# Values as the stationary operand, 64 columns a head, with attention outputs kept on chip in a one-core hybrid layer

## The chip, the cores and the metric

The kernel runs on one core of a Trainium2 chip. The metric is the device time of one execution in microseconds (us). The kernel before took 1282.35 us in the median of three runs (1281.9 to 1283.98). For one more execution the profiler recorded every instruction; all rows quoted below come from that one.

A core has five engines with a queue of instructions each, which the profile names PE (TensorE, matrix products), DVE (VectorE), ACT (ScalarE), POOL (GpSimd) and SP (SyncE, which here only issues DMAs). ACT issues some DMAs too. An engine executes its queue in order and waits on semaphores for others. A matrix product is two instructions on PE: a load of the stationary operand (PEld, LDWEIGHTS) and the streaming of the moving operand through it (PE, MATMUL). Results go to PSUM.

## What is computed

The layer has a convolution branch, an attention branch and a gated merge. The change lies in the attention branch, whose reference is this:

```python
scores = jnp.einsum('bdhnqe,bdhnke->bdhnqk', qb, kb) * (e ** -0.5)
scores = jnp.where(mask, scores, NEG_INF)
m = jnp.max(scores, axis=-1)
p = jnp.exp(scores - m[..., None])
den = jnp.sum(p, axis=-1)
o = jnp.einsum('bdhnqk,bdhnke->bdhnqe', p, vb) / den[..., None]
...
m_all = jnp.maximum(jnp.maximum(maxes[0], maxes[1]), maxes[2])
wts = [d_g * jnp.exp(m_g - m_all) for m_g, d_g in zip(maxes, dens)]
w_sum = wts[0] + wts[1] + wts[2]
att = (wts[0][..., None] * outs[0] + wts[1][..., None] * outs[1]
       + wts[2][..., None] * outs[2]) / w_sum[..., None]
y_att = (att * jax.nn.silu(z_att)) @ w_att_out[layer]
```

There are 1024 tokens and 24 heads of 64 channels: three groups of eight heads. Group g looks back over a window of 128 steps at a stride of 1, 4 or 16 tokens. Group 0 has one sequence of 1024 tokens, group 1 has four of 256, group 2 sixteen of 64, of which two share a tile of 128 queries. A query tile of 128 attends its own key block and, where there is one, the block before: 256 keys, or 128. The three outputs of a head position are merged by the softmax denominators and row maxima.

## The kernel before

Every float32 operand of a product is split in a high part, which the fast float32 format holds, and a low part, the rest. ACT writes the high part and DVE (or POOL, for some weights) the low one (`split`, L55 to L58). A projection takes three products (`mm3`, L73 to L75).

Attention is done for `order`: 12 units n = (j, g), j a pair of heads (0 to 3), g the group. One unit has two heads and eight query tiles a head; a **stage** is one pair of neighbouring tiles of one head, so a unit has 8 stages and the whole has 96. A loop over **slots** (at the end of `layer`) writes PE's order by hand; a slot is about 3.8 to 4.6 us long. A slot holds, in this order on PE:

- a piece of 12 products of 512 columns of a projection that runs beside attention (`pieces`): k and q of later units, then from slot 85 on the eight gate projections. `Parts` takes k and q out of PSUM with rotary, `gate` takes a gate out with a sigmoid on ACT;
- `scores(st)` of stage st = slot: q stationary, k moving, 2 products a tile. DVE adds the mask and takes the row extremum (L861, written to `ov`), ACT takes the exponential and the row sum (L865);
- `turn` of the stage two slots back (TURN = 2): transposes of the exponentials on PE (L873), then `split` into `ph` and `pl`;
- `values` of the stage three slots back (VAL = 3): for each query tile and key block two products (L886), `ph` and `pl` stationary with 128 columns, and v moving, 128 columns: 64 of the high part and 64 of the low part of one head. A DVE sum (L889) adds the two halves into the tile `ov`, which has tokens on partitions and 66 columns a head: 64 outputs, the sum, the extremum;
- work put into later slots by `beside`.

After the last stage of a unit `o_store` writes `ov` to DRAM (`oscr`), in token order, by ACT's queue. When the three groups of a pair j are there, `combine(j, half)` loads half the tokens back (`rd`, L898), forms the weights, sums the groups on DVE (L910 to L935), transposes the result with four PE transposes (L939) and multiplies it with the SiLU gate, which SP loads (`at`). For j < 3 the product goes to DRAM (`atscr`) and is read back after the last stage; for j = 3 it is split at once (`att_parts`).

`load_v(n)` reads v of one unit from DRAM (`vr`) and splits it in `vt`. `move_kq` moves k and q of a head within SBUF by 32-partition DMAs that SP issues (L794).

PE's order is the one in which the code is written; on DVE, ACT, POOL and SP the framework's scheduler places the instructions by its own estimates of time, within the data's dependences and the tiles' buffers. Each engine then keeps that order on the chip.

## Time and profile before

| what | us |
|---|---|
| three runs, median (lowest, highest) | 1282.35 (1281.9, 1283.98) |
| the profiled execution, own time | 1283.09 |
| its span, first to last instruction | 1281.3 |
| granted TensorE clock, share of full | 0.998 |
| first score product to last value product | 671.0 to 1090.4 |
| last of the gate projections ends | 1141.7 |

A row of the groups reads: line, engine, operation, output<-inputs by tile names, shapes, count | busy us, mean ns of one | idle time before them and what ended it. Matmul durations overlap each other, so a group's busy time is not the time that PE needs for it; that is the spacing from one start to the next, which the timeline shows. In the table of waits a row says who waited for whom, the total in us, how often, and the longest.

### The profile page before, as it was taken

To read this page: it belongs to the slowest core of one execution; us is meant where nothing else is said; L and a number is where in the kernel's file an instruction comes from. 1 tells how busy PE (TensorE), PEld (TensorE's weight loads), DVE (VectorE), ACT (ScalarE), POOL (GpSimd) and SP (SyncE) were. 2 spreads that over 40 slices of the span, in tenths; PEclk is the share of its full clock that TensorE was granted. 3 is DMA by queue.
4 is the path that set the end of the run, shared out by engine and by line. 5 is a ranking of instruction groups with operands and counts; after the bars stand their busy time and mean duration, and the time that the engine had idled before them with its cause. 6 is when DMAs were issued, how large, how long until landed. Compare 5 with 4: busy or idle time off the path is not lost. (4 is left out here: it accounts for less than half of the span.)

```text
span 1281.3 us, 16765 instructions
## 1 busy us (share of the span) xinstructions
PE 1250.6 (98%) x6148; PEld 1050.8 (82%) x6148; DVE 932.8 (73%) x1600; ACT 489.6 (38%) x957; POOL 91.8 (7%) x79
## 2 busy tenths in 40 slices
PE   6999999999999999999999999999999999999997
PEld 4777888888888888888788888888888888788886
DVE  6777999999999986853257667866876854448544
ACT  4653202111221156620125545545545567334211
POOL 0000000000000000000131111111011111100000
PEclk9999999999999999999999999999999999999999
DMA  9522311211211122555665556566565563648321
GB/s 366 189 90 72 109 66 60 89 51 48 92 57 50 50 74 74 166 178 187 147 166 128 149 149 175 151 168 168 152 186 143 152 203 106 205 168 307 100 99 66
DMA packets 85525, 171.52 MB, mean 134 GB/s; under 512 B 11202, under 2 KB 41026, under 8 KB 85444
## 3 DMA queue, kind: packets, MB, share of 16 engines
q1 hardware_dynamic: 69024, 157.66, 40.9%
q10 hardware_dynamic: 16420, 12.80, 3.3%
q8 instruction: 48, 0.79, 0.2%
q14 instruction: 33, 0.27, 0.1%
HBM read 105.74 MB, written 33.23 MB: 108 GB/s over the span
## 5 line engine op out<-in xcount | busy, mean ns | idle before, releaser
L73 PE MATMUL d<-hh,whi 128*128 128x512 f32 x1072 | 424.8, 396 | 1.8 <-ACT gs L740 0.9
L74 PE MATMUL d<-hl,whi 128*128 128x512 f32 x1072 | 417.8, 390 | 2.1 <-DVE hl L347 2.1
L75 PE MATMUL d<-hh,wlo 128*128 128x512 f32 x1072 | 418.1, 390 | 0.0
L406 DVE SCALAR_TENSOR_TENSOR v<-u,cw,v 128x1024 f32<-128x1024 f32 x232 | 280.7, 1284 | 0.0
L75 PEld LDWEIGHTS d<-hh,wlo 128*128 128x128 f32 x1072 | 201.2, 188 | 43.3
L74 PEld LDWEIGHTS d<-hl,whi 128*128 128x128 f32 x1072 | 201.7, 188 | 41.7 <-DVE hl L347 2.9
L73 PEld LDWEIGHTS d<-hh,whi 128*128 128x128 f32 x1072 | 201.6, 188 | 41.4 <-ACT gs L740 1.3
L57 ACT ACTIVATE whi<-wraw 128x512 fp32r<-128x512 f32 (+1 forms) x107 | 88.0, 833 | 252.0 <-PE d L74 227.1
L58 POOL TENSOR_TENSOR wlo<-wraw,whi 128x512 fp32r<-128x512 f32 (+1 forms) x56 | 82.7, 1490 | 668.0 <-ACT whi L57 625.1
L865 ACT ACTIVATE sb<-sb,ov 128x128 f32<-128x128 f32 (+1 forms) x192 | 84.6, 442 | 45.2 <-DVE ov L861 44.8
L861 DVE CUSTOM_DVE_ANT_0 sb<-s,mask 128x128 f32<-128x128 f32 (+1 forms) x192 | 59.8, 347 | 34.3 <-PE s L858 34.1
L58 DVE TENSOR_TENSOR pl<-t,ph 128x384 fp32r<-128x384 f32 (+2 forms) x96 | 52.2, 544 | 29.1 <-ACT ph L57 28.4
L886 PE MATMUL o<-vt,ph 128*128 128x128 f32 x280 | 71.1, 286 | 1.4 <-ACT ph L57 1.2
L886 PE MATMUL o<-vt,pl 128*128 128x128 f32 x280 | 68.1, 277 | 2.9 <-DVE pl L58 2.6
L58 DVE TENSOR_TENSOR wlo<-wraw,whi 128x1024 fp32r<-128x1024 f32 (+1 forms) x51 | 58.0, 1139 | 15.9 <-ACT whi L57 15.3
L57 ACT ACTIVATE ph<-t 128x384 fp32r<-128x384 f32 (+2 forms) x96 | 46.0, 480 | 58.8 <-PE t L873 56.5
L886 PEld LDWEIGHTS o<-vt,pl 128*128 128x128 f32 x280 | 53.7, 192 | 4.5 <-DVE pl L58 4.4
L886 PEld LDWEIGHTS o<-vt,ph 128*128 128x128 f32 x280 | 53.5, 191 | 2.9 <-ACT ph L57 2.8
L1089 PE MATMUL d<-oh,hl 128*128 128x512 f32 (+1 forms) x136 | 51.2, 376 | 0.0
L1087 PE MATMUL d<-oh,hh 128*128 128x512 f32 (+1 forms) x136 | 51.2, 376 | 0.0
L632 DVE TENSOR_TENSOR gs<-d,sgc 128x512 f32<-128x512 f32 x16 | 11.1, 692 | 54.9 <-PE d L75 48.9
L858 PE MATMUL s<-k,ql 128*128 128x128 f32 (+1 forms) x192 | 50.9, 279 | 0.0
(220 smaller groups left out, 1924.0 us busy)
## 6 DMA issues: line engine op xcount, KB each, us to landing
wraw<-in_w_t SPq DMA_DIRECT2D x67, 512.0 KB, 4.3
k<-kqp SPq DMA_DIRECT2D x96, 128.0 KB, 4.0
q<-kqp SPq DMA_DIRECT2D x96, 128.0 KB, 3.4
wa<-in_w_ada SPq DMA_DIRECT2D x16, 512.0 KB, 6.3
rd<-oscr SPq DMA_DIRECT2D x8, 792.0 KB, 4.9
ql<-kqp SPq DMA_DIRECT2D x48, 128.0 KB, 3.1
wraw<-in_w_v SPq DMA_DIRECT2D x11, 512.0 KB, 3.7
x<-in_xT SPq DMA_DIRECT2D x8, 512.0 KB, 10.2
```

The source lines that it names most:

```text
L57: nc.scalar.activation(hi, raw, AF.Copy)
L58: (lo_eng or nc.vector).tensor_sub(lo, raw, hi.bitcast(F32))
L73: nc.tensor.matmul(ps, lh, rh, start=start, stop=False)
L74: nc.tensor.matmul(ps, lh, rl, start=False, stop=False)
L75: nc.tensor.matmul(ps, ll, rh, start=False, stop=stop)
L406: nc.vector.scalar_tensor_tensor(d, u[:, k:k + S], cw[:, ct, k:k + 1], d, op0=mult, op1=add)
L858: nc.tensor.matmul(ps[:, c:c + w], ql[:, ts_], k[:, ks], start=False, stop=True)
L861: nc.vector.tensor_tensor_reduce(out=sb[:, c:c + w], in0=ps[:, c:c + w], in1=mk, scale=-SCALE, scalar=3e38, op0=add, op1=ALU.min, accum_ou ...
L865: nc.scalar.activation(sb[:, c:c + w], sb[:, c:c + w], AF.Exp, bias=ov[:, t, h, 65:66], scale=-1.0, accum_out=ov[:, t, h, 64:65])
L886: nc.tensor.matmul(self.po[:, t % 4], parts[x][:, c + i:c + i + P], v[:, kb], start=i == 0 and x == 0, stop=i + P == w and x == 1)
L1087: nc.tensor.matmul(ps, hh[:, k, c], rh, start=k == 0, stop=False)
L1089: nc.tensor.matmul(ps, hl[:, k, c], rh, start=False, stop=k == KT - 1)
```

## The change

In words:

- **values**: v is now stationary, 64 columns of one head, high or low part; `ph` and `pl` move. Per key block three products, vh·ph, vl·ph and vh·pl, are summed in PSUM; vl·pl is no longer formed. For groups 0 and 1 one key block serves its own query tile and the next, so one product moves 256 columns. The result lies in PSUM with the 64 channels on partitions and the tokens in columns.
- **outputs**: one ACT copy for two stages (64 partitions by 512) puts them into a tile `oc` that holds two heads (partitions 0 to 63 and 64 to 127) by 1024 tokens and stays in SBUF. The DVE sum is gone, and so are `oscr` and the load `rd`.
- **statistics**: sums and extrema lie in a tile `stats`, which ACT's queue stores to `sscr` (16 bytes a token, group and pair). `combine(j)`, once for all 1024 tokens, loads them (`sd`), forms 48 columns of weights, transposes these on PE (one transpose), stores them to `wscr` and loads them back as rows, broadcast over 64 partitions (`wg`, six pairs of loads). The products with the weights run on `oc` in place. Group 1 and 2 are read in token order through the access pattern.
- **buffers**: `wg`, the gate (`gt`), `row`, `w` and `wt` share one tag of two buffers; `oc` has four.
- **v** is loaded and split in two halves of four key blocks each, later than before.
- **order**: VAL is 4, and `values` stands before `turn` in a slot.

The diff, cut:

```diff
+    sscr = [dram.tile([S, 3, 4], F32, name=f"sscr{j}") for j in range(4)]
+    wscr = [dram.tile([3, 2, S], F32, name=f"wscr{j}") for j in range(4)]
...
-    oscr = [dram.tile([S, 3, 2 * 66], F32, name=f"oscr{j}") for j in range(4)]
...
         for h in range(2):
-            v = v2[n, h] = stk.tile([P, 8, P], F32R, name="vt", tag=f"v{turn_of(n, h)}")
-            src = raw[:, :, 64 * h:64 * h + 64]
-            nc.scalar.activation(v[:, :, 0:64], src, AF.Copy)
-            nc.vector.tensor_sub(v[:, :, 64:128], src, v[:, :, 0:64].bitcast(F32))
+            if not half:
+                v2[n, h] = stk.tile([P, 8, 2, 64], F32R, name="vt", tag=f"v{turn_of(n, h)}")
+            hi, lo = (v2[n, h][:, 4 * half:4 * half + 4, x] for x in range(2))
+            split(hi, lo, raw[:, :, 64 * h:64 * h + 64])
             yield
...
         def values(self, st_):
             tp, h, spans, _ = self.spans(st_)
-            parts, v = self.pt.pop(st_), v2[self.n, h]
+            (ph, pl), v = self.pt.pop(st_), v2[self.n, h]
             if st_ % 2 == 0:
-                self.po = psa.tile([P, 4, P], F32, name="o", tag="o")
-            for t, c, w in spans:
-                for i in range(0, w, P):
-                    kb = t - (w - P - i) // P
-                    for x in range(2):
-                        nc.tensor.matmul(self.po[:, t % 4], parts[x][:, c + i:c + i + P], v[:, kb],
-                                         start=i == 0 and x == 0, stop=i + P == w and x == 1)
+                self.po = psa.tile([P, 512], F32, name="o", tag="o")
+
+            c, w = spans[0][2] - P, (1 if self.g == 2 else 2) * P
+            blocks = [(tp, c, w, 0), (tp + 1, c + w, P, P)]
+            if c:
+                blocks.insert(1, (tp - 1, 0, P, 0))
+            for n, (kb, c, w, q) in enumerate(blocks):
+                out_ = self.po[0:64, tp % 4 * P + q:tp % 4 * P + q + w]
...
+                nc.tensor.matmul(out_, v[:, kb, 0], ph[:, c:c + w], start=first_, stop=False)
+                nc.tensor.matmul(out_, v[:, kb, 1], ph[:, c:c + w], start=False, stop=False)
+                nc.tensor.matmul(out_, v[:, kb, 0], pl[:, c:c + w], start=False, stop=last_)
             if st_ % 2:
-                nc.vector.tensor_reduce(self.ov[:, tp - 2:tp + 2, h, 0:64],
-                                        self.po.rearrange("p t (x c) -> p t c x", x=2),
-                                        axis=mybir.AxisListType.X, op=add)
...
+                nc.scalar.activation(self.o[64 * h:64 * h + 64, (tp - 2) * P:(tp + 2) * P], self.po[0:64], AF.Copy)
...
+    def combine(j):
+        sd = ap_.tile([P, 8, 3, 2, 2], F32, name="sd")
+        nc.sync.dma_start(sd.rearrange("p t g h x -> p t (g h x)"), sscr[j].rearrange("(t p) g c -> p t (g c)", p=P))
...
+        nc.scalar.activation(m, m, AF.Exp, scale=-1.0)
...
+        nc.tensor.transpose(pt[0:48, 0:P], w, ident)
+        wt = row_tile("wt")[0:48, 0:P]
+        nc.scalar.activation(wt, pt[0:48, 0:P], AF.Copy)
+        nc.sync.dma_start(wscr[j].rearrange("g h (t p) -> (g h t) p", p=P), wt)
...
+            for h in range(2):
+                nc.sync.dma_start(row[64 * h:64 * h + 64], wscr[j][g, h:h + 1, s].to_broadcast([64, 512]))
...
+        for half, s in enumerate(halves):
...
+            nc.vector.tensor_mul(o0, o0, w0)
+            w2 = row_of(2, s)
+            v = w1.rearrange("p (i r) -> p i r", r=4)
+            nc.vector.tensor_mul(v, v, o1)
+            nc.vector.tensor_add(o0, o0, w1)
+            gt = row_tile("gt")
+            nc.sync.dma_start(gt, zascr[j][:, s])
+            yield
+            v = w2.rearrange("p (i t s) -> p i t s", t=8, s=2)
+            nc.vector.tensor_mul(v, v, o2)
+            nc.vector.tensor_add(o0, o0, w2)
+            nc.vector.tensor_mul(o0, o0, gt)
...
-    LEAD, TURN, VAL = 11, 2, 3
+    LEAD, TURN, VAL = 11, 2, 4
...
-    FIRST, SECOND = (2, 6, 6, 7, 7, 9), (8, 11, 11, 12, 12, 14)
+    STEPS = (2, 3, 4, 5, 7, 8, 9, 10, 11)
```

What it does to PE's order shows in a slot of the fifth unit (j = 1, g = 1), whose stage has three key blocks in all. Before, from the scores on (k and q are the score operands, t the transposes, o the values):

```order
L857 MATMUL s<-k_5847,q_5848 128x128
L858 MATMUL s<-k_5847,ql 128x128
L857 MATMUL s<-k_5847,q_5848 128x256
L858 MATMUL s<-k_5847,ql 128x256
L873 MATMUL t<-ident,sb 128x128 x3
L886 MATMUL o<-vt,ph 128x128
L886 MATMUL o<-vt,pl 128x128
L886 MATMUL o<-vt,ph 128x128
L886 MATMUL o<-vt,pl 128x128
L886 MATMUL o<-vt,ph 128x128
L886 MATMUL o<-vt,pl 128x128
```

Now, from the last score on, for the same pair of tiles:

```order
L863 MATMUL s<-k_5728,ql 128x256
L896 MATMUL o<-ph,vt 64x256
L897 MATMUL o<-ph,vt 64x256
L898 MATMUL o<-pl,vt 64x256
L896 MATMUL o<-ph,vt 64x128
L897 MATMUL o<-ph,vt 64x128
L898 MATMUL o<-pl,vt 64x128
L878 MATMUL t<-ident,sb 128x128 x4
```

The last name in a row is the stationary operand: six products with 128 stationary columns became six with 64, three of them twice as wide in the moving operand, and the transposes moved behind them (they belong to another stage, so their count differs). Over all stages 560 value products of 128 columns became 456 of 128 and 192 of 256, and 32 transposes in `combine` became 4.

The second place is SP's queue in the first `combine` (j = 0), from the first broadcast rows of its first half to its last store; k and q belong to the sixth unit. None of the `wg` rows stood there before; `rd`, `at` and `atscr` did:

```order
L941 DMA wg<-wscr_97 64x512 [waits DMAHW1_49,DMAHW5_49,DMAHW0_49,DVE_49]
L941 DMA wg<-wscr_97 64x512 [waits DMAHW6_49]
L794 DMA k_6154<-kqp 32x1024 [waits DMAHW7_49,DVE_49]
L959 DMA gt<-zascr_89 128x512 [waits DMAHW3_49,DMAHW2_49,DVE_49]
L794 DMA q_6155<-kqp 32x1024 x2
L794 DMA ql<-kqp 32x1024
L941 DMA wg<-wscr_97 64x512 [waits DMAHW5_49,DMAHW6_49,DMAHW4_49,DVE_49]
L941 DMA wg<-wscr_97 64x512
L941 DMA wg<-wscr_97 64x512 [waits DMAHW0_49,DVE_49]
L941 DMA wg<-wscr_97 64x512 [waits DMAHW7_49]
L968 DMA atscr_101<-oc 128x512
```

Each load that reuses a buffer waits for the DVE operation which read it last, and the moves of k and q stand between those waits.

The third place is ACT's queue at the end of the last unit, where the statistics of the last pair are stored and loaded (`ph` are the last exponentials on their way to the values, `gs` a gate projection):

```order
L701 DMA sscr_96<-stats 512x1x4 [waits Activation_49]
L701 DMA sscr_96<-stats 512x1x4
L57 ACTIVATE whi<-wraw 128x1024 [waits DMAHW0_49,PE_49,Pool_49]
L740 ACT_TABLE_LOAD [waits DMAHW5_49]
L740 ACTIVATE gs<-d 128x512 [waits PE_49]
L57 ACTIVATE ph<-t 128x256 [waits PE_49]
L741 DMA ascr<-gs 128x512 [waits Activation_49]
L57 ACTIVATE ah<-wraw 128x512 [waits DMAHW0_49]
L921 ACT_TABLE_LOAD [waits DMAHW2_49]
L921 ACTIVATE sd<-sd 128x48 [waits DVE_49]
L902 ACTIVATE oc<-o 64x512 [waits PE_49]
L57 ACTIVATE ph<-t 128x256 [waits PE_49]
```

The exponential of the merged statistics of the last pair (L921), which waits for a store and a load, now stands ahead of the last `ph` of the program; before, that of the last pair (L916) stood behind all `ph`.

## The prediction

> **What bounds the kernel now.** I began with the totals of the page.

> ```profile
> span 1281.3 us, 16765 instructions
> PE 1250.6 (98%) x6148; PEld 1050.8 (82%) x6148; DVE 932.8 (73%) x1600; ACT 489.6 (38%) x957; POOL 91.8 (7%) x79
> ```

> PE is busy for 98% of the span; no other engine is near. So the time is the number of products times the spacing from one start to the next, plus the few places where PE waits. Next I read PE's timeline of one slot of group 2, for the spacing (start, duration, engine, line):

> ```profile
> 764.10 0.39 PE L75 MATMUL d<-hh,wlo 128*128 128x512 f32 x1
> 764.32 0.22 PE L857 MATMUL s<-k,q 128*128 128x128 f32 x1
> 764.38 0.28 PE L858 MATMUL s<-k,ql 128*128 128x128 f32 x1
> 764.49 0.27 PE L857 MATMUL s<-k,q 128*128 128x128 f32 x1
> 764.61 0.28 PE L858 MATMUL s<-k,ql 128*128 128x128 f32 x1
> 764.72 0.40 PE L873 MATMUL t<-ident,sb 128*128 128x128 f32 x2
> 764.88 0.31 PE L886 MATMUL o<-vt,ph 128*128 128x128 f32 x1
> 765.02 0.27 PE L886 MATMUL o<-vt,pl 128*128 128x128 f32 x1
> 765.13 0.27 PE L886 MATMUL o<-vt,ph 128*128 128x128 f32 x1
> 765.24 0.28 PE L886 MATMUL o<-vt,pl 128*128 128x128 f32 x1
> 765.36 0.45 PE L73 MATMUL d<-hh,whi 128*128 128x512 f32 x1
> ...
> 765.87 0.39 PE L75 MATMUL d<-hh,wlo 128*128 128x512 f32 x1
> 766.10 0.39 PE L73 MATMUL d<-hh,whi 128*128 128x512 f32 x1
> ```

> Products of 512 columns start 0.23 us apart (765.87 to 766.10). The value products, 128 moving columns each with a stationary operand of its own, start 0.11 us apart. But the first score product needed only 0.06 us (764.32 to 764.38): the load of the next operand had been done under the 512 columns ahead. So 128 columns stream in about 58 ns, and what holds the value products at 112 ns is the load of 128 stationary columns. The next timelines, PEld and then a score stage with 256 moving columns, say the same:

> ```profile
> 764.43 0.19 PEld L857 LDWEIGHTS s<-k,q 128*128 128x128 f32 x1
> 764.54 0.19 PEld L858 LDWEIGHTS s<-k,ql 128*128 128x128 f32 x1
> ...
> 766.10 0.19 PEld L74 LDWEIGHTS d<-hl,whi 128*128 128x128 f32 x1
> ```

> ```profile
> 783.74 0.28 PE L857 MATMUL s<-k,q 128*128 128x256 f32 x1
> 783.85 0.28 PE L858 MATMUL s<-k,ql 128*128 128x256 f32 x1
> 783.97 0.28 PE L857 MATMUL s<-k,q 128*128 128x256 f32 x1
> 784.09 0.28 PE L858 MATMUL s<-k,ql 128*128 128x256 f32 x1
> ```

> Loads follow each other at 0.11 us (764.43, 764.54), and 256 moving columns cost 0.12 us, hardly more than 128. Last, the table of PEld's waits in the attention stretch (in all, times, longest):

> ```profile
> PEld o L886 <- DVE pl L58: 4.4, 11, 0.8
> PEld o L886 <- ACT ph L57: 2.8, 6, 1.1
> PEld s L857 <- DVE ov L861: 2.8, 1, 2.8
> PEld d L73 <- ACT gs L740: 1.3, 1, 1.3
> ```

> Most of what PE loses there, 7.2 us, is the value products waiting for `pl` and `ph`.

> **Value products.** Nothing in the trace loads 64 columns. Two rows give load durations for 2 columns and for 128:

> ```profile
> L320 PEld LDWEIGHTS d<-wh,s_parts x8: 83/83/83, 95.8 to 99.0; 128*2 128x2 f32 x8
> L125 PEld LDWEIGHTS d<-ones,tot x32: 188/192/192, 47.4 to 489.2; 128*128 128x128 f32 x32
> ```

> That is (188 - 83) / 126 = 0.83 ns a column; 64 columns fewer take 53 ns off the 112, which leaves 59 ns, as much as the 58 ns of the stream. Bounds for a product of 64 by 128: 57 ns (the stream alone) and 112 ns (no price by column); with 256 moving columns 113 to 120 ns. I take 59 and 120, near the lower end, because the 2-column load, 105 ns shorter, shows that a load does get shorter with its columns. [...]

> By stage, before against after:
> - 24 stages of four blocks: 8 x 112 = 896 ns; now three products of 256 and six of 128, 3 x 120 + 6 x 59 = 714. Saving 182 ns, 4.4 us in all.
> - 40 of three blocks: 6 x 112 = 672; now 3 x 120 + 3 x 59 = 537. Saving 135 ns, 5.4 us.
> - 32 of two blocks (group 2): 4 x 112 = 448; now 6 x 59 = 354. Saving 94 ns, 3.0 us.

> That makes 12.8 us. By the halves of a ns that the rows don't resolve (58 to 66 for the 128) it lies between 13.4 and 9.6; I take **11.4** (62 ns).

> **Transposes in combine.**

> ```profile
> L939 PE MATMUL t<-ident,pr 128*128 128x128 f32 x32 | 4.9, 277 | 0.0
> ```

> These 32 become 4. They too load one operand each, so 28 x 0.11 = **3.1 us** less on PE.

> **The later values.** VAL = 4 leaves `ph` and `pl` one more slot, about 4 us, against waits of 1.1 us at most: I take off all **7.2 us**. What is late next is the pair that the table names besides, the extrema (2.8 us, at the first stage, where k and q arrive) and `gs` (1.3 us); both stay.

> **DVE and ACT.** These are off the path:

> ```profile
> L889 DVE TENSOR_REDUCE ov<-o 128x256 f32<-128x512 f32 x48 | 32.7, 682 | 1.4 <-PE o L886 1.1
> L510 ACT ACTIVATE gs<-d 128x512 f32<-128x512 f32 x24 | 14.2, 592 | 21.8 <-issue 14.5 <-PE d L75 7.3
> L930 DVE TENSOR_TENSOR rd<-rd,w 128x512 f32<-128x512 f32 x24 | 17.4, 777 | 0.0
> ```

> DVE loses the 48 sums, 32.7 us. ACT gains 48 copies out of PSUM, 0.59 us each by the row of `gs` (the same shape), 28 us. The merge itself keeps about its work: twelve products and sums of 128 by 512 a pair at 0.78 us are 9.3 us; before, `rd` alone had 24 / 4 = 6 of them a pair beside other, smaller ones. Strided reads of `oc` may cost more, up to the 1.03 us of the dearest 128x512 operation on DVE, 3 us a pair. I cost this at nothing, since DVE has room; the next windows show it (span, PE, PEld, DVE, ACT, POOL busy, clock, DMA share, GB/s), first between two `combine`s, then where the gates run:

> ```profile
> 772.00:875.00 103.00, 102.14 (x606) 89.50 (x605) 76.17 (x226) 53.57 (x155) 15.33 (x12) 1.00 0.63 167
> 1048.00:1064.00 16.00, 15.49 (x93) 13.15 (x92) 5.77 (x23) 12.87 (x28) 2.40 (x1) 1.00 0.44 124
> ```

> DVE has 103 - 76 = 27 us free. ACT has 49 us free in the first stretch, but only 3.1 of 16 us in the second.

> **SP and the moves.** In the new order SP's queue holds the broadcast rows, `gt` and the moves of k and q, each load waiting for DVE to be done with a buffer. Without k and q I count 28 issues a pair instead of 13.

> ```profile
> 834.16 1.23 SPq L794 DMA_DIRECT2D q<-kqp  x2
> ...
> SPq L942 <- DVE at L940: 24.5, 5, 8.0
> ...
> at<-zascr SPq DMA_DIRECT2D x8, 256.0 KB, 3.6
> row<-bscr SPq DMA_DIRECT2D x8, 64.0 KB, 4.0
> ```

> At 1.23 / 2 = 0.62 us an issue that is 15 x 0.62 = 9 us more of SP's time in about 103 us. SP already stood still for up to 8.0 us behind DVE in `combine`, and no wait of PE for k or q came of it after the first stage. So nothing for that, unless DVE itself gets stuck (below).

> **New waits.** `combine` now makes a chain: `sd` load, DVE, exponential, DVE, PE transpose, store, broadcast load, DVE. A load takes 3.6 to 4.0 us by the rows above. At the end of the last unit the exponential stands ahead of the last `ph` on ACT, behind a store and a load; and `combine`'s DVE rows stand in front of the extrema and of `pl`. Neither has a row in the trace; below, the cost is nothing if the load lands in time; above, one store and one load, about 8 us, less the 4 us which VAL gives. I take **2 us**, the middle; a gain is excluded, because the old order had no such wait.

> **Sum.** The profiled execution took 1283.09 us (span 1281.3 and 1.8 around it). 1283.1 - 11.4 - 3.1 - 7.2 + 2.0 = 1263.4. The median of the runs is 0.7 below the profiled one: **1262.7 us**. With the kindest bounds (13.4 and no new wait) 1258.7; with the waits of the first stage and of `gs` gone as well, 1254.6. With 9.6 and 4 us of waits 1266.5.

> **Rivals.**
> 1. *The load has no price by column.* Then 128 moving columns cost 112 still, and the extra products are a loss: four blocks 3 x 120 + 6 x 112 = 1032 against 896, three 696 against 672, two 672 against 448; 3.3 + 1.0 + 7.2 = 11.5 us more instead of 11.4 less. 1262.7 + 22.9 = 1285.6, and some less where a load hides beside 256 columns: 1281 to 1286, no change to slightly slower. Against it: the 83 ns of L320.
> 2. *Loads don't run under a product whose rows they share.* Each product would take load plus stream: 456 x 0.117 + 192 x 0.179 = 87.7 us instead of 560 x 0.112 = 62.7: 25 more; 1262.7 + 36.4 = 1299. Against it speaks that at 766.10 a load and a 512-column product, both on all 128 rows, start together and products stay 0.23 us apart. [...]
> 3. *DVE gets stuck in `combine`* (slower). Four waits a half for rows or gate, eight a pair, at 4 us: 32 us in which DVE, in order, does neither extrema nor `pl`. `STEPS` spreads `combine` over ten slots, about 42 us at 4.2; there DVE has a quarter free, 11 us, and four of the 0.68 us sums less, 3 us; PE follows some 6 us later by the slots between scores and values. 32 - 11 - 3 - 6 = 12 us a pair, three pairs: 36 us, 1299. It decides once DVE falls over 6 us behind. For it: two buffers for everything, each load issued only when its buffer is free. Against it: the pieces of `combine` stand in separate slots, 4 us apart, so that a load has landed by the next piece. A partial form costs 5 to 15 us: 1268 to 1278.
> 4. *ACT becomes the bound where the gates run.* 12.87 of 16 us there, plus a copy each 2 slots (0.59 in about 8 us, 1.2 in 16): 88%. Table loads on top can make ACT late for `ph` in the last 11 slots, at 0.5 us each 5 us: 1268.

> **How the numbers follow.** Chances: the forecast 0.70 (1255 to 1268), ACT 0.10 (1268), DVE stuck 0.10 (half 1268 to 1278, half beyond), load without a price by column 0.07 (1281 to 1286), serial load 0.03 (1299). The range 1255 to 1276 leaves out the last two, most of the far half of the third and a little below. A measurement of this kernel can tell 0.2%, 2.6 us, from no change. Faster by more than that (below 1279.8): 0.70 + 0.10 + 0.05 = 0.85; within it 0.06, most of rival 1; slower 0.09, rivals 2, half of 3 and a rest of 1.

> **What would show it.** On PE, the value products L896 to L898 should start 58 to 66 ns apart with 128 moving columns, 120 with 256; at 112 rival 1 holds, at 117 and 179 rival 2. PEld's waits for `ph` and `pl` should be gone; if they stand with more than 2 us, the term of 7.2 is wrong, and ACT's share in the gates' slots tells rival 4. For rival 3 look at waits of PE for extrema and `pl` while DVE waits for `wg` or `gt`. Wrong altogether would be a PE busy time that didn't fall by some 14 us.

## The result and the profile after

The changed kernel takes 1287.13 us in the median of seven runs (1282.65 to 1289.57), the kernel before 1282.35. The ratio is 1.0034, with a 95% interval of 1.0017 to 1.0050: slower by a third of a per cent, where 1.5% faster was forecast. The profiled execution took 1287.98 us, its span and totals are:

```profile
span 1286.2 us, 16854 instructions
PE 1243.6 (97%) x6208; PEld 1041.9 (81%) x6208; DVE 915.3 (71%) x1496; ACT 516.6 (40%) x1027; POOL 94.7 (7%) x79
```

PE's busy time fell by 7 us, not by the 14 that the prediction named as its sign, and the span grew by 4.9; so PE waits more, and some of its products run slower. First the products. This is PE's timeline of a slot of group 1 in the changed kernel, with no wait in it:

```profile
724.40 0.28 PE L896 MATMUL o<-ph,vt 128*64 128x256 f32 x1
724.52 0.28 PE L897 MATMUL o<-ph,vt 128*64 128x256 f32 x1
724.63 0.28 PE L898 MATMUL o<-pl,vt 128*64 128x256 f32 x1
724.75 0.22 PE L896 MATMUL o<-ph,vt 128*64 128x128 f32 x1
724.80 0.22 PE L897 MATMUL o<-ph,vt 128*64 128x128 f32 x1
724.86 0.23 PE L898 MATMUL o<-pl,vt 128*64 128x128 f32 x1
```

With 128 moving columns the value products start 0.05 to 0.07 us apart, with 256 some 0.116. Over the attention stretch the median spacings are 60 and 116 ns: 456 x 0.060 + 192 x 0.116 = 49.6 us, against 62.7 before. Their loads last 134 ns by the next group, between the 83 of 2 columns and the 188 of 128:

```profile
L898 PEld LDWEIGHTS o<-pl,vt 128*64 128x64 f32 x216 | 29.0, 134 | 0.3 <-DVE pl L58 0.3
```

That is (134 - 83) / 62 = 0.82 ns a column, the price that was taken. So 13.1 us are saved on values and 28 x 0.11 = 3.1 on transposes.

Then PEld's waits from 630 to 1200 us, after:

```profile
PEld s L862 <- issue: 6.1, 2, 3.1
PEld d L73 <- ACT gs L740: 4.7, 2, 3.8
PEld o L897 <- DVE vt L58: 4.3, 3, 1.7
PEld t L932 <- DVE pl L58: 3.7, 3, 1.4
...
PEld o L896 <- ACT ph L57: 1.6, 1, 1.6
...
PEld o L896 <- ACT vt L57: 0.9, 1, 0.9
```

The waits for `pl` and `ph` went from 7.2 to 1.9 us, as forecast. But new ones stand there: scores without k and q ("issue", 6.1), values without v (5.2), the one transpose of `combine` (3.7), and `gs` at the end (4.7 instead of 1.3). With the rows left out the table sums to 26.2 us against 13.2 before.

Last, the clock. The windows give, as columns, PE, PEld, DVE, ACT and POOL busy, granted clock, DMA share, GB/s. One row of before, where every such window from 640 to 1200 us has a clock of 1.00, then the four of after that have less:

```profile
1040.00:1080.00 40.00, 38.47 (x224) 32.93 (x222) 14.53 (x54) 29.20 (x64) 4.79 (x2) 1.00 0.44 128
```

```profile
680.00:720.00 40.00, 39.34 (x237) 34.61 (x238) 24.38 (x70) 24.39 (x66) 5.12 (x4) 0.96 0.53 124
920.00:960.00 40.00, 35.72 (x210) 30.59 (x210) 29.12 (x73) 20.51 (x61) 6.25 (x4) 0.96 0.61 167
1040.00:1080.00 40.00, 37.26 (x211) 31.95 (x212) 13.86 (x60) 33.05 (x73) 4.78 (x2) 0.92 0.60 169
1080.00:1120.00 40.00, 36.58 (x180) 29.86 (x180) 13.17 (x26) 21.15 (x36) 7.15 (x3) 0.96 0.49 142
```

PE's timeline after the wait for q and k at 942 us shows what a lower clock looks like:

```profile
948.46 0.63 PE L75 MATMUL d<-hh,wlo 128*128 128x512 f32 x1
948.88 0.63 PE L73 MATMUL d<-hh,whi 128*128 128x512 f32 x1
```

Products start some 0.43 us apart; from 950.74 on it is 0.23 again. From 640 to 1200 us 29 pairs of neighbours stand 0.40 to 0.45 us apart after, none before, and others are slowed in part. By the windows the lost clock is 40 x (0.04 + 0.04 + 0.08 + 0.04) = 8 us. Slower products also count as busier (0.63 us each where 0.39 is usual), which is, as an estimate, why PE's busy time fell by 7 us and not by 14. So the account is -13.1 - 3.1 + 13.0 + 8 = +4.8 us, and the span grew by 4.9.

By place (from the start of the first score product of one slot to that of another; the runs of the experiments stand with them):

| slots | before | after | `gt_pool` | `no_wg` |
|---|---|---|---|---|
| 0 to 24 (first pair) | 100.9 | 99.4 | 99.4 | 99.2 |
| 27 to 41 (`combine` of pair 0) | 63.6 | 63.8 | 59.9 | 63.9 |
| 41 to 51 (no `combine`) | 39.2 | 38.4 | 38.4 | 38.4 |
| 51 to 65 (`combine` of pair 1) | 63.6 | 66.7 | 65.5 | 62.1 |
| 75 to 89 (`combine` of pair 2) | 63.7 | 64.4 | 64.2 | 60.2 |
| from 95 to the end | 201.8 | 205.1 | 207.6 | 206.7 |

Where no `combine` runs, the kernel gains; where one runs, it loses that and more, and the end loses 3.3 us.

### The profile page after: what moved, and what is told of

It reads as the page before. It is cut to its first block, busy times and chain, and to the rows that moved or that the text cites. A ratio compares the mean times of both kernels' runs of the same rounds, so it can differ in the third digit from the quotient of the medians.

```text
span 1286.2 us, 16854 instructions
## 1 busy us (share of the span) xinstructions
PE 1243.6 (97%) x6208; PEld 1041.9 (81%) x6208; DVE 915.3 (71%) x1496; ACT 516.6 (40%) x1027; POOL 94.7 (7%) x79
## 4 chain that ended last, share of the span: by engine, by line
PE 81%; DVE 7%; ACT 5%; DMA 4%; issue 2%; ACTq 0%; SPq 0%; DVEq 0%
PE d L73 19%; PE d L74 19%; PE d L75 19%; PE d L1113 2%; PE d L1112 2%; PE d L467 2%; PE d L1111 2%; PE d L469 2%; PE d L468 2%; PE t L878 1%; ACT sb L870 1%; PE d L251 1%; PE s L863 1%; PE d L249 1%; PE d L250 1%
## 5 line engine op out<-in xcount | busy, mean ns | idle before, releaser
L73 PE MATMUL d<-hh,whi 128*128 128x512 f32 x1072 | 430.6, 402 | 4.8 <-ACT gs L740 3.9
L74 PE MATMUL d<-hl,whi 128*128 128x512 f32 x1072 | 420.4, 392 | 1.7 <-DVE hl L349 1.7
L75 PE MATMUL d<-hh,wlo 128*128 128x512 f32 x1072 | 420.8, 393 | 0.0
L408 DVE SCALAR_TENSOR_TENSOR v<-u,cw,v 128x1024 f32<-128x1024 f32 x232 | 280.5, 1278 | 0.0
L73 PEld LDWEIGHTS d<-hh,whi 128*128 128x128 f32 x1072 | 203.3, 190 | 45.3 <-ACT gs L740 4.7
L75 PEld LDWEIGHTS d<-hh,wlo 128*128 128x128 f32 x1072 | 202.8, 189 | 43.7
L74 PEld LDWEIGHTS d<-hl,whi 128*128 128x128 f32 x1072 | 203.7, 190 | 42.0 <-DVE hl L349 2.5
L57 ACT ACTIVATE whi<-wraw 128x512 fp32r<-128x512 f32 (+1 forms) x107 | 88.1, 834 | 238.1 <-PE d L74 219.0
L58 POOL TENSOR_TENSOR wlo<-wraw,whi 128x512 fp32r<-128x512 f32 (+1 forms) x56 | 85.7, 1542 | 669.7 <-ACT whi L57 629.1
L870 ACT ACTIVATE sb<-sb,stats 128x128 f32<-128x128 f32 (+1 forms) x192 | 85.0, 444 | 121.4 <-DVE stats L866 121.2
L58 DVE TENSOR_TENSOR pl<-t,ph 128x384 fp32r<-128x384 f32 (+2 forms) x96 | 52.3, 545 | 104.5 <-ACT ph L57 104.3
L58 DVE TENSOR_TENSOR wlo<-wraw,whi 128x1024 fp32r<-128x1024 f32 (+1 forms) x51 | 57.9, 1137 | 14.4 <-ACT whi L57 13.6
L862 PE MATMUL s<-k,q 128*128 128x128 f32 (+1 forms) x192 | 47.4, 270 | 7.6 <-DMA sscr<-stats 5.3
L897 PE MATMUL o<-ph,vt 128*64 128x128 f32 (+1 forms) x216 | 49.3, 239 | 3.5 <-DVE vt L58 3.5
L896 PE MATMUL o<-ph,vt 128*64 128x128 f32 (+1 forms) x216 | 49.1, 238 | 2.1 <-ACT ph L57 1.4
L634 DVE TENSOR_TENSOR gs<-d,sgc 128x512 f32<-128x512 f32 x16 | 11.1, 691 | 54.9 <-PE d L75 54.9
L467 PE MATMUL d<-vh,hh 128*128 128x512 f32 x128 | 49.8, 389 | 0.0
L468 PE MATMUL d<-vl,hh 128*128 128x512 f32 x128 | 49.8, 389 | 0.0
```

Of the source, the lines that this page charges most:

```text
L57: nc.scalar.activation(hi, raw, AF.Copy)
L58: (lo_eng or nc.vector).tensor_sub(lo, raw, hi.bitcast(F32))
L73: nc.tensor.matmul(ps, lh, rh, start=start, stop=False)
L74: nc.tensor.matmul(ps, lh, rl, start=False, stop=False)
L75: nc.tensor.matmul(ps, ll, rh, start=False, stop=stop)
L408: nc.vector.scalar_tensor_tensor(d, u[:, k:k + S], cw[:, ct, k:k + 1], d, op0=mult, op1=add)
```

## What stands behind the new waits

One of the two waits for k and q, from 839.6 to 842.2 us, is of scores whose operands haven't arrived. SP's queue ahead of it (start, duration of the issue):

```profile
827.25 0.34 SPq L959 DMA_DIRECT2D gt<-zascr  x1
...
828.21 0.59 SPq L794 DMA_DIRECT2D q<-kqp  x1
832.41 0.34 SPq L968 DMA_DIRECT2D atscr<-oc  x1
...
835.14 1.15 SPq L794 DMA_DIRECT2D k<-kqp  x2
836.34 1.22 SPq L794 DMA_DIRECT2D q<-kqp  x2
837.94 0.51 SPq L794 DMA_DIRECT2D ql<-kqp  x1
```

SP stands twice: from 825.1 to 827.25 at the load of `gt`, whose buffer DVE's L957 has to free, and from 828.8 to 832.4 at the store to `atscr`, which DVE's product with the gate (L964) releases. DVE's timeline, and what POOL does meanwhile:

```profile
825.55 1.67 DVE L957 TENSOR_TENSOR oc<-oc,wg 128x512 f32<-128x512 f32 x1
...
827.70 1.63 DVE L962 TENSOR_TENSOR wg<-wg,oc 128x512 f32<-128x512 f32 x1
...
831.38 0.40 DVE L58 TENSOR_TENSOR vt<-vr,vt 128x256 fp32r<-128x256 f32 x1
831.71 0.67 DVE L964 TENSOR_TENSOR oc<-oc,gt 128x512 f32<-128x512 f32 x1
832.31 0.41 DVE L58 TENSOR_TENSOR vt<-vr,vt 128x256 fp32r<-128x256 f32 x1
```

```profile
824.50 3.87 POOL L58 TENSOR_TENSOR wlo<-wraw,whi 128x512 fp32r<-128x512 f32 x2 [16.02 <-ACT whi L57]
```

The last moves of k and q for the next unit are in order behind that. They are issued at 835.1 to 838.4 us, and the last one lands at 842.5, while PE could start the scores at 839.5. Before, the same moves left at 829.0 to 832.1 and had landed by some 836, and PE came to these scores at 842.7. So the last move leaves 6.4 us later and PE comes 3.2 us earlier; together they use up the 6 to 8 us that lay between landing and use.

The low part of v (831.38, 832.31), for which PE waits at 830.9, is late for another reason. Its load had landed at 826.67. ACT wrote the high part at 828.7 to 829.4, behind exponentials that waited for DVE's extrema, and DVE came to the low part behind its merge, whose operations took longer than usual: 1.67 us for L957 and 1.63 for L962 where 0.69 and 1.09 are usual. POOL worked on `wlo`, the low part of a projection's weights, at just that time. In the two other `combine`s it is the same: L956 and L957 take 1.93 and 1.67 us at 927 to 931, L957 takes 2.78 at 1034.4, each beside `wlo` on POOL, and a wait for v comes behind each. The long operations also hold up SP, which waits for them. In all 15 runs whose merge has these operations, 64 of 696 took over 0.3 us longer than usual; each of the 64 ran beside a `wlo` of POOL for at least 0.45 us, while 27 others ran beside one without getting longer. This is a reading of traces: no run moved POOL's work.

The later values are the second thing. `ph` and `pl` may now be a slot later, and they are. For the 96 stages I took the time from the start of the last transposes to the end of `pl`: its median is 2.5 us before and 4.3 after, its maximum 5.9 and 9.6. Two rows of before and the same two of after, ACT's and DVE's waits in attention:

```profile
ACT sb L865 <- DVE ov L861: 44.8, 49, 3.0
DVE pl L58 <- ACT ph L57: 28.4, 26, 3.6
```

```profile
ACT sb L870 <- DVE stats L866: 121.2, 80, 3.5
DVE pl L58 <- ACT ph L57: 104.3, 71, 4.4
```

ACT now writes `ph` behind the exponentials of a later stage, these wait for DVE's extrema, and DVE, in order, waits for `ph`. Both spend time waiting for each other. In quiet slots PE doesn't wait for that; that it is this time which is missing when `combine` comes on top is an argument, which no run isolates.

## The experiments

Each was timed beside the kernel before on the same chip; before was 1282.5 to 1283.7 us there.

| run | median us | ratio to before, 95% interval |
|---|---|---|
| `b_val4` | 1288.16 | 1.0037 (1.0023 to 1.0050) |
| `val3` | 1285.48 | 1.0014 (1.0004 to 1.0024) |
| `no_wg` | 1274.11 | 0.9930 (0.9913 to 0.9946) |
| `wg_pool` | 1290.19 | 1.0054 (1.0039 to 1.0069) |
| `mv_pool` | 1294.70 | 1.0085 (1.0070 to 1.0100) |
| `t_in_s` | 1287.02 | 1.0029 (1.0017 to 1.0040) |
| `v_head` | 1300.78 | 1.0124 (1.0107 to 1.0141) |
| `all4m` | 1305.35 | 1.0168 (1.0153 to 1.0183) |
| `gt_pool` | 1281.50 | 0.9985 (0.9971 to 0.9999) |
| `late` | 1289.60 | 1.0054 (1.0034 to 1.0074) |
| `wg1` | 1363.72 | 1.0633 (1.0617 to 1.0649) |
| `sp_manual` | 1287.90 | 1.0041 (1.0025 to 1.0057) |
| `gp_ts` | 1281.10 | 0.9984 (0.9974 to 0.9993) |
| `gp_ts_tail` | 1281.05 | 0.9985 (0.9973 to 0.9996) |
| `gp_val3` | 1286.46 | 1.0023 (1.0009 to 1.0036) |
| `b_val4_s` | 1289.35 | 1.0043 (1.0030 to 1.0056) |

**The order alone.** In the kernel before, and taken back in the changed one:

```diff
-    LEAD, TURN, VAL = 11, 2, 3
+    LEAD, TURN, VAL = 11, 2, 4
...
-            if TURN <= slot_ < stages + TURN:
...
             if VAL <= slot_ < stages + VAL:
...
+            if TURN <= slot_ < stages + TURN:
```

> The kernel before with the new order alone: VAL = 4 and `values` ahead of `turn`; v stays moving. Theory (the later values take the 7.2 us of waits for `ph` and `pl` off PE, as predicted): 1282.4 - 5 to 7 = 1275 to 1277 us, PEld's waits at L886 under 1 us. Rival (DVE and ACT use the extra slot to write `ph` and `pl` later, so the wait moves along or turns into another): 1281 to 1283 us.

> The changed kernel with the old order: VAL = 3 and `turn` ahead of `values`. Theory (the new order saves the waits for `ph` and `pl`, the loss comes from elsewhere): 3 to 8 us above the changed kernel's 1287.1, 1290 to 1295, with 4 us or more of waits for `ph` and `pl` back. Rival (the new order is what hurts: it makes `t` come free late and moves the tail by a slot): under 1287, down to 1280, with the waits of L932 (3.5 us) and of `gs` (4.7 us) gone.

`b_val4` is 5.7 us slower than before. PEld's waits in it:

```profile
PEld t L939 <- DVE pl L58: 7.2, 4, 2.3
PEld t L873 <- DVE pl L58: 2.8, 2, 1.5
```

The waits for `ph` and `pl` are gone (0.7 us left) and 10 us stand at the transposes: their PSUM tile `t` is the one that `pl` of the slot before still has to read. The rival holds in its mechanism; its 1281 to 1283 was too low. But the waits of PE sum to 14.8 us, hardly more than the 13.2 of before, so they are not where most of the 5.7 us went. They are fewer and longer, up to 2.3 us where those for `ph` and `pl` lasted 1.1 at most. The granted clock of its five runs is 0.994 to 0.996, that of before 0.997 to 0.999, and its trace has three stretches of 3.4 us at half clock between 640 and 1200 us where before has none: some 5 us (estimate: half of each). One of the three follows the wait at the first stage, which before has too. By this estimate the order costs here mostly by the clock.

Taking the order back in the changed kernel did not make it 3 to 8 us slower. Its median is 2 us lower, which is not clear of the noise (the intervals overlap): waits for `pl` (8.6) and `ph` (4.2) return, those for k and q and for `t` go.

The same with the transposes of `combine` in another PSUM tile, to take that buffer out of the way:

```diff
-        pt = psa.tile([P, 512], F32, name="t", tag="t")
+        pt = psa.tile([P, 512], F32, name="s", tag="s")
```

> The kernel before in the new order (VAL = 4, `values` first), with the four transposes of `combine` in a PSUM tile `s` instead of `t`. Theory (the order fails because `pl` reads `t` a slot later): the waits of L939, 7.2 us, go, and with them half clock: 1278 to 1282 us, no better than before by 7. Rival (the backlog shows in another place of the same slots): 1285 to 1288.

The wait for `t` is gone, and the time is not (1289.35):

```profile
PEld s L857 <- DVE ov L861: 12.8, 4, 4.6
```

2.8 of it stood there before; 10 us have moved on to the scores, which now wait for DVE's extrema. So not the buffer but DVE, late in the slots of `combine`, is behind it: the removed wait shows up at the next thing that DVE owes.

**The buffer in the changed kernel.** The same edit at L931.

> The changed kernel with the transposed weights of `combine` in a PSUM tile of the scores (`s`) instead of one of the transposes (`t`). Theory (L932 waits because the `t` buffer of the slot before is read by `pl` only a slot later): its three waits, 3.5 us, go: 1282 to 1285 us. Rival (it waits for the weights `w` themselves): no change, 1286 to 1288.

The three waits of L932 went, and the time stayed: waits for v (7.0 us), `ph` (2.6) and extrema (3.6) are 3.6 us longer than in the changed kernel. The buffer was the cause of that wait, but taking it away gained nothing.

**The broadcast rows.** Without their loads:

```diff
-            for h in range(2):
-                nc.sync.dma_start(row[64 * h:64 * h + 64], wscr[j][g, h:h + 1, s].to_broadcast([64, 512]))
...
-            nc.vector.tensor_mul(o0, o0, w0)
+            nc.vector.tensor_mul(o0, o0, ctab[:, s])
```

> The changed kernel without the 48 loads of the broadcast rows `wg`: the merge multiplies with the resident cosine table instead of the weights (same DVE operations). Theory (SP's queue, stuck on `wg`, brings k and q of the next unit late, 6.2 us, and v late, 4.9 us): both waits go, with part of the time at the lower clock: 1276 to 1281 us. Rival (DVE's own backlog delays them, SP only follows): the waits stay, 1285 to 1288 us.

1274.1 us, 13 below the changed kernel and below what was expected. No wait for k, q or v is left in its PEld table. DVE's work is nearly the same (270.7 us busy between 671 and 1090, against 272.8), so the loads and the waiting for them are what the merge costs. With them gone the long merge operations go too: what they take above the usual sums to 2.1 us instead of 7.0. From POOL's queue instead:

```diff
-                nc.sync.dma_start(row[64 * h:64 * h + 64], wscr[j][g, h:h + 1, s].to_broadcast([64, 512]))
+                nc.gpsimd.dma_start(row[64 * h:64 * h + 64], wscr[j][g, h:h + 1, s].to_broadcast([64, 512]))
```

(and `gt`, `atscr` likewise)

> The changed kernel with the loads of `wg` and `gt` and the store to `atscr` issued from POOL's queue instead of SP's; nothing is left out. Theory (SP's queue): as without the loads, 1276 to 1282 us, unless POOL, waiting in order, brings the low weights late. Rival (the round trips hold up DVE itself): 1285 to 1290 us.

The waits for k, q and v went here too, as the theory says; but the time is no better than that of the changed kernel (3 us more in the median, not clear of the noise), with 11.4 us of waits for `pl` (the longest 5.3) and 8.3 for `gs`. DVE waits for the rows themselves now:

```profile
DVE oc L953 <- DMA wg<-wscr: 7.2, 4, 2.4
```

It waits for rows for 13.5 us in all, against 2.6 in the changed kernel. So once SP's queue is free the round trip of the rows holds up DVE; but from POOL's queue the rows also land more slowly, in 3.7 us (median) instead of 3.0, and this run can't separate the two.

How steep waiting for rows can be, `wg1` shows. It writes each pair of loads as one, with a leading dimension of 2:

```diff
-            for h in range(2):
-                nc.sync.dma_start(row[64 * h:64 * h + 64], wscr[j][g, h:h + 1, s].to_broadcast([64, 512]))
+            nc.sync.dma_start(row, wscr[j][g, :, s].unsqueeze(1).to_broadcast([2, 64, 512]))
```

> The changed kernel with each pair of broadcast loads of `wg` written as one load: 24 issues instead of 48, the same bytes and the same waits for buffers. Theory (SP's standing still counts, not the issues): the waits for k, q and v stay, 1284 to 1288 us. Rival (the issues themselves, 0.6 us each, 15 us in all, make SP late): the waits shrink by more than half, 1278 to 1282.

It was meant to tell issues from waiting, and doesn't, because the load itself became slow: one issued at 813.0 us was there at 822.7, with DVE waiting for it for 5.3 us, where a load of the changed kernel lands in 3.0 (median). DVE waits:

```profile
DVE wg L955 <- DMA wg<-wscr: 35.4, 8, 5.2
DVE wg L961 <- DMA wg<-wscr: 31.9, 7, 5.4
DVE oc L952 <- DMA wg<-wscr: 27.8, 6, 9.3
```

95 us of waiting on DVE made the kernel 77 us slower. That is the mechanism of the prediction's third rival; its full form was priced at 36 us. Why a load with a leading dimension of 2 lands so late, no run shows.

**The moves of k and q on POOL's queue.**

```diff
-        nc.sync.dma_start(dst[row + 32 * part:row + 32 * part + 32].bitcast(F32), src.bitcast(F32))
+        nc.gpsimd.dma_start(dst[row + 32 * part:row + 32 * part + 32].bitcast(F32), src.bitcast(F32))
```

> The changed kernel with the moves of k and q issued from POOL's queue; `wg`, `gt`, `atscr` and v stay on SP. Theory (k and q stand behind `gt` and `atscr` in SP's queue): the two waits of L862 for k and q, 6.2 us, go, and about 2 us of half clock after the second: 1277 to 1281 us. Rival (the moves are late because DVE writes `kqp` late): the waits stay, 1285 to 1288. If POOL, waiting in order for a move, brings `wlo` late, L75 or L74 shows waits for POOL.

A miss: 7.6 us slower. The moves land in 3.6 to 4.6 us (medians of k, q and `ql`) instead of 2.6 to 2.8, POOL is busy 170 of 419 us between 671 and 1090 instead of 67, and DVE waits more for rows:

```profile
DVE oc L953 <- DMA wg<-wscr: 17.7, 3, 6.4
```

The waits for k and q are gone but for 1.3 us at the very first scores, and waits for `ph` (11.1), `pl` (7.0) and extrema (7.2) take their place. The trace shows why. The rows are issued at once when the store of the weights (`wscr`) has landed, and this store takes 6.8, 6.1 and 6.5 us in the three `combine`s instead of 2.8, 1.4 and 1.4; SP stands from 794.7 to 801.2 for it. In the first two, POOL has issued seven moves in the 3.5 us before. In the first `combine` the rows come no later than in the changed kernel (801.3 and 801.8 us); there DVE's order has L953 12 us earlier (798.7 instead of 810.9), and DVE stands. So 240 transfers less on SP's queue gained nothing for a store that lands late behind them.

**v by head.** Loaded and split a head at a time, earlier:

```diff
-        return [8 * n + x for x in ((2, 4, 5) if half else (-2, 0, 1))]
+        return [8 * n + x for x in ((0, 2) if half else (-4, -2))]
```

> The changed kernel with v loaded by head (all 8 key blocks of 64 channels) instead of by halves of the key blocks: a head is loaded 8 slots before its first use and split 6 before, instead of 6 and 4 for the first half, and 4 and 2 for the second. Theory (v comes late by its load's place in SP's queue): the waits of L896 and L897 for `vt`, 4.9 us, go and about 1.5 us of half clock: 1280 to 1283 us. Rival (DVE's backlog only moves to another operand): waits for `pl` or k and q grow by as much, 1285 to 1288.

The waits for v went, as expected, and the kernel became 13.7 us slower than the changed one. PE's waits, and SP's queue ahead of the first of them, which lasts from 836.2 to 844.1 us:

```profile
PEld s L859 <- DVE rot L723: 16.0, 2, 8.1
PEld s L859 <- issue: 7.3, 1, 7.3
```

```profile
833.58 1.28 SPq L688 DMA_DIRECT2D vr<-vscr  x2
...
836.08 1.19 SPq L794 DMA_DIRECT2D k<-kqp  x2
839.00 1.14 SPq L794 DMA_DIRECT2D q<-kqp  x2
```

PE comes to these scores 3 us earlier than in the changed kernel, and k and q leave 1 to 3 us later, behind `atscr` (issued at 832.6) and now a load of v too: three waits of 7 to 8 us, one a pair. The first row names DVE's `rot`, but that had been written at 843.3 at the latest; what PE waited for was q, which landed at 843.9. The move of k took 6.8 us to land, behind two loads of weights. That supports SP's queue as the cause.

**These together**, and the work after the last stage a slot earlier (`j = slot_ - stages - 3`):

> The three edits together (moves on POOL, weights in `s`, v by head), and the work after the last stage (`ah`, `oh`) one slot earlier, as before the change. Theory (the waits are separate causes and add up): 6.2 + 3.5 + 4.9 us of waits and half of the 7 us at half clock go: 1268 to 1272 us, below both kernels. Rival (one backlog, that of DVE around `combine`, lies behind all of them): over 1278.

1305.35: the rival. Nothing added up; waits for `ph`, `pl` and extrema sum to 27.6 us.

**Only the last two transfers of a half on POOL's queue.**

```diff
-            nc.sync.dma_start(gt, zascr[j][:, s])
+            nc.gpsimd.dma_start(gt, zascr[j][:, s])
...
-                nc.sync.dma_start(atscr[j][:, s], o0)
+                nc.gpsimd.dma_start(atscr[j][:, s], o0)
```

> The changed kernel with only the loads of `gt` and the stores to `atscr` on POOL's queue; `wg`, v and the moves of k and q stay on SP. Theory (what holds k and q up is that SP stands still at `gt` and `atscr` until DVE is done with the last products of `combine`): the two waits of L862, 6.2 us, go, and about 1 to 2 us of half clock: 1279 to 1282 us. Rival 1 (the number of issues on SP, mostly `wg`, is what costs): 1284 to 1288. Rival 2 (POOL's queue hurts as it did with `wg` on it): over 1288, with waits for `pl` or `gs`.

1281.5, 5.6 below the changed kernel and as expected: 14 transfers out of SP's way, and the "issue" row for k and q and the rows for `vt` are gone. In the first `combine` the 14 slots take 59.9 us instead of 63.8, 3.7 under the kernel before; in the two others it gains only 1.2 and 0.2. There a merge operation is long again beside `wlo` on POOL (927.2 to 929.7 us):

```profile
927.14 3.49 DVE L962 TENSOR_TENSOR wg<-wg,oc 128x512 f32<-128x512 f32 x1
```

In the third `combine` the same operation takes 3.22 us from 1030.93, beside `wlo` from 1030.8 to 1033.2; in the first it took 1.60. PE waits right behind both: 2.0 us for extrema and 1.5 for `pl`, and 2.4 for `pl`.

**Other orders on SP.** `late` writes the loads of the third row and the gate a slot behind the DVE operations that free their buffers; `sp_manual` keeps SP in written order:

```diff
-    STEPS = (2, 3, 4, 5, 7, 8, 9, 10, 11)
+    STEPS = (2, 3, 4, 5, 6, 7, 8, 9, 10, 11, 12)
```

```diff
-    with tc.manual_schedule(engines={nc.tensor.engine}):
+    with tc.manual_schedule(engines={nc.tensor.engine, nc.sync.engine}):
```

> The changed kernel with `combine` cut in smaller steps, a slot each: the loads of the third row and of `gt` are written one slot behind the DVE operations that free their buffers, the end lies one slot later. Nothing is left out. Theory (SP stands still because each load is written right behind the DVE operation that it waits for): waits for k, q and v shrink by half or more, 1278 to 1283 us. Rival (SP is late because DVE is, by slots): 1285 to 1290.

> The changed kernel with SP's queue in the order in which the code is written, as PE's is, instead of the scheduler's. The loads of v then stand ahead of the second `atscr`, and k and q still stand behind `gt` and `atscr`. Theory (standing still at these two decides): the waits for k and q stay, those for v shrink at best: 1283 to 1289 us. Rival (the scheduler's order of SP is what hurts): under 1281.

`late` is a miss, and its rival holds: v is waited for 0.3 us instead of 5.2, but k and q 8.2 instead of 6.1. The second `atscr` of each pair leaves at 831.6, 937.4 and 1041.1 us, in the same slots as in the changed kernel, and k and q still stand behind it. `sp_manual` lies in the range of its theory, but not by its mechanism: the waits for v didn't shrink but grew to 8.7 us, some 7 stand at the first scores of a unit, and 9.8 near the end are for weights that are split late.

**Combined.** `gp_ts` is `gt_pool` with `t_in_s`; `gp_ts_tail` has the end a slot earlier as well; `gp_val3` is `gt_pool` in the old order.

> The changed kernel with both edits: `gt` and `atscr` on POOL's queue, and the transposed weights in a PSUM tile `s`. Theory (two separate waits): the 3.5 us of L932 come off the 1281.5 of the first edit: 1276 to 1279 us, below both kernels. Rival (the wait moves to `pl` or k and q of the same slots): 1280 to 1283.

> The same, with the work after the last stage (`ah`, `oh`) one slot earlier, as it stood before the change. Theory (`gs`, 5.9 us of waits, is late because ACT waits in order for a load of `oh`, and these are a slot late): 2 to 4 us less than without it, 1273 to 1277 us. Rival (the loads wait for buffers anyway): no difference, 1276 to 1280.

> The changed kernel with `gt` and `atscr` on POOL's queue and the old order (VAL = 3, `turn` first). Theory (the extra slot is taken up by later `ph` and `pl`, so the order is worth little either way): 1278 to 1283 us, with 6 to 13 us of waits for `ph` and `pl` and none for `t`. Rival (the new order is worth what was forecast once SP is freed): 1286 to 1290.

`gp_ts` equals `gt_pool` (1281.1 and 1281.5): the wait for `t` is gone once more and `pl` takes its place, 7.1 us instead of 4.4. The rivals of both hold, the second but for 1 us of its number. The end a slot earlier brought nothing in the median (1281.05), though its profiled execution has 4.0 instead of 6.3 us of waits for `gs`. `gp_ts` and `gp_ts_tail` are below both kernels, by some 0.15% under the one before. `gp_val3` went against my theory and as its rival said: with SP freed, the old order is 5 us worse (1286.5), with 16.7 us of waits for `pl` and `ph`. The waits explain only part of it: of the 3.5 us between the two profiled spans they make 1.7 (24.4 against 22.7 us in all) and the clock none; the rest lies in the spacing of products and in waits too short for the table. So the new order is worth some 5 us in that kernel and costs 6 in the one before; in the changed one, with SP blocked, the 2 us that it seems to cost are not clear of the noise.

## Why the prediction failed

- **Value products**: right in mechanism, mis-sized by little: 11.4 us forecast, 13.1 by the spacings, because both came near their lower bounds (60 and 116 ns, bounds 57 and 113). The measured 0.82 ns a column agrees with the 60 ns: by this estimate a load of 64 columns, 52 ns, would be hidden under a stream of 58, a quarter of the 0.23 us between products of 512 columns. The rivals on the load are excluded. **Transposes**: 3.1, right.
- **The later values**: the step that failed first. "I take off all 7.2 us" counted the extra slot as slack. `b_val4` alone gives +5.7 us: `ph` and `pl` are placed up to a slot later, PE waits elsewhere instead (`t`, then the extrema), as long in all but in longer pieces, and by the estimate above these cost clock (granted 0.994 to 0.996 against 0.997 to 0.999). In the changed kernel 5.3 of the 7.2 did go, and others came.
- **SP and the moves**: "nothing for that" was wrong by 6.1 us of waits for k and q. The prediction had counted the issues and seen that SP had stood still for 8 us without harm; but that stop, from 839.7 to 847.8 us, began when the next unit's k and q had left. It hadn't asked how long before their use they were issued. The last one now leaves 6.4 us later, behind the stops at `gt` and `atscr`, and PE comes 3.2 us earlier, because it saves time on the values. `gt_pool`, which takes just these transfers out of the way, is 5.6 us faster and has no such wait.
- **DVE and ACT**: "I cost this at nothing, since DVE has room" was wrong by most of the 5.2 us of waits for v. DVE has room in the mean, but v's low part stands in its order behind merge operations of 1.6 to 2.8 us, longer than the dearest that the prediction allowed for (1.03). They ran beside `wlo` on POOL; that this is their cause is read from the traces and not tested.
- **New waits**: 2 us forecast. The sum of the new rows is 19 us, most of it the two above. The end, where 2 us were expected, lost 3.3.
- **The third rival** (DVE stuck in `combine`) had the right engine and the wrong form: DVE itself waited for rows only 2.6 us; its lateness travelled by SP's queue to k and q, and along its own order to v. `no_wg` prices the loads of the rows, with what comes of them, at 13 us.
- **The clock** was in no term: 8 us, in five stretches at half clock, each behind 1.6 to 2.9 us without a product.

What stays open: whether POOL's work is what makes DVE's merge long (a run with `wlo` on another engine or in other slots would tell), and why the moves of k and q and the store land later when POOL issues the moves. A third buffer for the rows wasn't tried.

## What to carry to other kernels

A span of 98% PE says what bounds the mean, not what bounds the slots in which a helper like `combine` runs: there DVE, ACT and a DMA queue were a few us from taking over, and the time saved on PE was spent waiting for them. Before crediting a removed wait, ask which order will use up the slack; before adding loads to a shared in-order queue, look up how long ahead of their use the transfers behind them are issued now. And see how long PE's waits are, not only what they sum to: in `b_val4` nearly the same sum (14.8 us against 13.2) in longer pieces (at the transposes up to 2.3 us, where those for `ph` and `pl` had lasted 1.1 at most) came with a lower clock as well (0.994 to 0.996 against 0.997 to 0.999).

## What the runs showed of the hardware

So it matters where a wait falls on the grid. After the wait for k and q of 2.6 us at 839 no clock was lost: a border at 841.2 cut it, and the windows on its sides had 1.53 and 1.10 us. The wait for q and k at 942 to 945.5 left 2.18 us in one window, and the next, from 947.0, ran at half clock. The wait at the first stage, some 2.3 us, left 2.34 us in one window in the changed kernel, and half clock followed. In the kernel before it is cut and left 1.74 us at most, and none followed (its grid is taken from its only stretch, at 1275.6 us). So part of the lost clock is luck of where the grid lies.
